# Rotating 96 images by 180 degrees on one core: a group of images is every third image instead of 32 in a row

## The chip, the cores and the metric

The kernel runs on one core of one Trainium2 chip. The metric is the device time of one execution in microseconds. A core has several engines that run side by side; this kernel uses VectorE (DVE in the profile) to copy, SyncE (SP) and ScalarE (ACT) only to issue transfers, and 16 DMA engines that move the bytes between the off-chip memory (HBM, called DRAM in the program) and the on-chip memory (SBUF, 128 partitions).

## The reference

The input is 32 x 3 images of 256 x 256 float32. Each image is turned by 180 degrees, that is, reversed in both of its last dimensions:

```python
batch, c, h, w = 32, 3, 256, 256
return np.rot90(x, k=2, axes=(-2, -1)).astype(np.float32)
```

Seen as a row of 65,536 numbers, an image is simply reversed. 96 images of 256 KB are 25.17 MB, to be read once and written once.

## The kernel before

Each image is cut into 4 quarters of 64 KB (E = 16,384 numbers). A group is 32 images, so it has 128 quarters, one for each SBUF partition. There are three groups, and one buffer for each: A, Bt and Ct (128 x 64 KB each). Partition p holds quarter p modulo 4 of the group's image p // 4.

In the off-chip memory, group 0 is images 0 to 31, group 1 is images 32 to 63, group 2 the rest. The view x4 (lines 37 and 38) joins image and quarter to one dimension of 128 rows, which lie 64 KB apart: a group is one stretch of 8 MB. The view o4 (lines 39 and 40) keeps image and quarter apart, because the store writes the quarters of each image in reversed order (line 59, `::-1`).

The numbers within a quarter are reversed by VectorE in place. `swap` (line 61) exchanges a piece at the left with its mirror piece at the right, in three copies by way of a small buffer T, each reading backwards. A group takes four swaps of 2048 numbers (12 copies of line 52).

The transfers are issued in this order. ScalarE issues the load of the first 512 numbers of each row of A. SyncE issues the load of the rest of A, of Bt, and of Ct, all at the start; line 55 is the call. Then SyncE issues the stores (line 58), each after the copies that it needs: a lead store of the first 128 numbers of each row of A, which can go once the first swap is done; the rest of A; Bt; Ct. VectorE swaps A but for a last piece (1152 numbers), then all of Bt, then A's last piece, then Ct. All DMAs of one issuing engine form one queue, and each of the 16 DMA engines works through its share in order.

Of the kernel before, what the change touches and what calls it, by code (L numbers as in the profile page):

```python
# [2 lines left out]

os.environ.setdefault("NEURON_RT_ULTRASERVER_MODE", "4")

# [4 lines left out]


@with_exitstack
def kernel(
    ctx: ExitStack,
    tc: tile.TileContext,
    x: bass.AP,
    out: bass.AP,
):

    nc = tc.nc
    P = 128

    B, C, H, W = x.shape
    L = H * W
    G = 32
    E = L // 4
    J = E // 8

    x4 = x.rearrange("b c h w -> (b c) (h w)").rearrange(
        "(g n) (s e) -> g (n s) e", n=G, s=4)
    o4 = out.rearrange("b c h w -> (b c) (h w)").rearrange(
        "(g n) (s e) -> g n s e", n=G, s=4)  # L40

    pool = ctx.enter_context(tc.tile_pool(name="slots", bufs=1))
    A = pool.tile([P, E], x.dtype, tag="A")
    Bt = pool.tile([P, E], x.dtype, tag="B")
    Ct = pool.tile([P, E], x.dtype, tag="C")
    T = pool.tile([P, J], x.dtype, tag="T")

    def back(t, lo, hi):
        return t[:, hi - 1:(lo - 1 if lo else None):-1]

    def copy(dst, src):
        tc.keep_in_program_order(nc.vector.tensor_copy(out=dst, in_=src))  # L52

    def load(t, g, lo, hi, queue=nc.sync):
        return queue.dma_start(out=t[:, lo:hi], in_=x4[g][:, lo:hi])  # L55

    def store(t, g, lo, hi):
        return nc.sync.dma_start(
            out=o4[g][:, ::-1, lo:hi], in_=t[:, lo:hi])

    def swap(t, lo, w):
        hi = E - lo - w
        copy(T[:, 0:w], back(t, hi, hi + w))
        copy(t[:, hi:hi + w], back(t, lo, lo + w))
        copy(t[:, lo:lo + w], T[:, 0:w])

    def inside(t):
        for lo in range(0, E // 2, J):
            swap(t, lo, J)

    HEAD = 512
    load(A, 0, 0, HEAD, nc.scalar)
    load(A, 0, HEAD, E)
    load(Bt, 1, 0, E)
    load(Ct, 2, 0, E)
    LAST = 1152
    LEAD = 128
    for lo in range(0, E // 2 - J, J):
        swap(A, lo, J)
    swap(A, E // 2 - J, J - LAST)  # L80
    store(A, 0, 0, LEAD)
    inside(Bt)
    swap(A, E // 2 - LAST, LAST)
    store(A, 0, LEAD, E)
    store(Bt, 1, 0, E)
    inside(Ct)
    store(Ct, 2, 0, E)


# [1 line left out]
_INS = ['x']  # L91
_OUTS = [((32, 3, 256, 256), 'float32')]


# [23 lines left out]
```

## Time and profile before

| what | value |
|---|---|
| median of 3 runs | 121.98 us (121.88 to 122.0) |
| the profiled execution, its time | 122.03 us |
| its span, first to last instruction | 120.2 us |
| VectorE busy | 44.6 us, 37% of the span, 39 copies with 3 waits for loads |
| wait of the first copy of A, of Bt, of Ct for its load | 22.7, 6.1, 1.9 us |
| DMA | 1152 packets, 50.33 MB, 419 GB/s over the span |

The profile's times count from the start of the span. A DMA has an issue, which is the time that an instruction takes on SyncE's or ScalarE's queue, and packets, which are the rows that the DMA engines move afterwards. Here a packet is a row of up to 64 KB. In the slices and windows, a packet counts where it begins, so figures of short stretches scatter around the mean.

### The profile page before, as it was taken

Reading aid. Unit: us, or ns where it says so; the run is one execution under the profiler, and the core shown is the slowest. Engines: PE = TensorE matmul, PEld = TensorE weight load, DVE = VectorE, ACT = ScalarE, POOL = GpSimd, SP = SyncE. Lnnn points to the kernel's source line nnn. Section 1 sums busy time; section 2 is a strip of 40 time slices with the busy share of each in tenths; the row PEclk is TensorE's granted clock in tenths of the full one; section 3 lists DMA queues with packets and bytes.
Section 4 is the critical chain, followed back from the end, with each engine's and each line's share of the span. In section 5 each row is a group of like instructions: output and inputs, shape, how many; then the busy total and the mean of one; then the engine's idle time right before and its main releaser. Section 6 shows DMA issues by size and latency. Waiting matters only on the chain.

```text
span 120.2 us, 98 instructions
## 1 busy us (share of the span) xinstructions
DVE 44.6 (37%) x39; POOL 0.2 (0%) x4
## 2 busy tenths in 40 slices
DVE  0000000499990099999759999400000000000000
POOL 0000000000000000000000000000000000000000
DMA  9888988899889988998889777988898889888980
GB/s 338 349 349 349 698 349 349 360 654 392 349 349 610 436 349 349 589 458 349 349 368 692 346 346 346 692 349 349 349 698 349 349 349 698 349 349 349 676 371 0
DMA packets 1152, 50.33 MB, mean 419 GB/s; under 512 B 128, under 2 KB 256, under 8 KB 384
## 3 DMA queue, kind: packets, MB, share of 16 engines
q1 hardware_dynamic: 1008, 50.07, 96.7%
q10 hardware_dynamic: 144, 0.26, 0.6%
HBM read 25.17 MB, written 25.17 MB: 419 GB/s over the span
## 4 chain that ended last, share of the span: by engine, by line
DMA 34%; DVE 27%; another core or an unknown queue 2%; issue 1%; SPq 0%; DVEq 0%
DMA Bt<-in_x_dram 34%; DVE T L52 9%; DVE Bt L52 8%; DVE Ct L52 8%; DVE A L52 1%; SPq L55 0%; DVEq L52 0%
## 5 line engine op out<-in xcount | busy, mean ns | idle before, releaser
L52 DVE COPY T<-A 128x2048 f32<-128x2048 f32 (+2 forms) x5 | 5.1, 1014 | 22.8 <-DMA A<-in_x_dram 22.7
L52 DVE COPY T<-Bt 128x2048 f32<-128x2048 f32 x4 | 4.9, 1227 | 6.2 <-DMA Bt<-in_x_dram 6.1
L52 DVE COPY T<-Ct 128x2048 f32<-128x2048 f32 x4 | 4.9, 1227 | 2.0 <-DMA Ct<-in_x_dram 1.9
L52 DVE COPY A<-T 128x2048 f32<-128x2048 f32 (+2 forms) x5 | 5.1, 1013 | 0.2
L52 DVE COPY A<-A 128x2048 f32<-128x2048 f32 (+2 forms) x5 | 5.1, 1013 | 0.2
L52 DVE COPY Bt<-T 128x2048 f32<-128x2048 f32 x4 | 4.9, 1227 | 0.1
L52 DVE COPY Ct<-T 128x2048 f32<-128x2048 f32 x4 | 4.9, 1227 | 0.1
L52 DVE COPY Bt<-Bt 128x2048 f32<-128x2048 f32 x4 | 4.9, 1226 | 0.1
L52 DVE COPY Ct<-Ct 128x2048 f32<-128x2048 f32 x4 | 4.9, 1226 | 0.1
L102 POOL MEMSET const-bfloat16-1.0<- 128x1 bf16 x1 | 0.1, 103 | 0.0
L102 POOL MEMSET const-uint8-127<- 128x1 uint8 x1 | 0.1, 103 | 0.0
L102 POOL MEMSET const-float32-1.0<- 128x1 f32 x1 | 0.1, 100 | 0.0
L102 POOL MEMSET const-float32-0.0<- 128x1 f32 x1 | 0.1, 99 | 0.2 <-issue 0.2
## 6 DMA issues: line engine op xcount, KB each, us to landing
out_dram<-A SPq DMA_DIRECT2D x1, 8128.0 KB, 21.2
A<-in_x_dram SPq DMA_DIRECT2D x1, 7936.0 KB, 21.9
A<-in_x_dram ACTq DMA_DIRECT2D x1, 256.0 KB, 22.1
out_dram<-A SPq DMA_DIRECT2D x1, 64.0 KB, 35.2
Bt<-in_x_dram SPq DMA_DIRECT2D x1, 40.8
Ct<-in_x_dram SPq DMA_DIRECT2D x1, 59.8
out_dram<-Bt SPq DMA_DIRECT2D x1, 39.9
out_dram<-Ct SPq DMA_DIRECT2D x1, 42.8
```

The lines of the kernel that those rows point to most:

```text
L52: tc.keep_in_program_order(nc.vector.tensor_copy(out=dst, in_=src))
L102: nc = _bacc.Bacc("TRN2", target_bir_lowering=False, num_devices=1)
```

## The change

A group becomes every third image: group 0 is images 0, 3, 6, and so on, group 1 is 1, 4, 7, group 2 is 2, 5, 8. Both views are changed alike, so what is loaded as one group is stored to its own place again. Consecutive images of a group then lie 768 KB apart instead of 256 KB; the four quarters of an image stay next to each other. Image and quarter can no longer be joined to one dimension of equal steps, so x4 keeps them apart and the load names one dimension more.

```diff
     x4 = x.rearrange("b c h w -> (b c) (h w)").rearrange(
-        "(g n) (s e) -> g (n s) e", n=G, s=4)
+        "(n g) (s e) -> g n s e", n=G, s=4)
     o4 = out.rearrange("b c h w -> (b c) (h w)").rearrange(
-        "(g n) (s e) -> g n s e", n=G, s=4)
+        "(n g) (s e) -> g n s e", n=G, s=4)
...
     def load(t, g, lo, hi, queue=nc.sync):
-        return queue.dma_start(out=t[:, lo:hi], in_=x4[g][:, lo:hi])
+        return queue.dma_start(out=t[:, lo:hi], in_=x4[g][:, :, lo:hi])
```

## The prediction

> **What bounds the kernel now.** I read the busy shares first, then the DMA queues and the windows, then the timeline of the issues, and the chain of waits last. The page (span, busy times, queues):
>
> ```profile
> span 120.2 us, 98 instructions
> DVE 44.6 (37%) x39; POOL 0.2 (0%) x4
> ...
> DMA  9888988899889988998889777988898889888980
> ...
> q1 hardware_dynamic: 1008, 50.07, 96.7%
> q10 hardware_dynamic: 144, 0.26, 0.6%
> HBM read 25.17 MB, written 25.17 MB: 419 GB/s over the span
> ```
>
> VectorE works 37% of the span; the 16 DMA engines carry packets for 96.7 + 0.6 = 97.3% of it. The windows show that their rate has a ceiling and sits on it in both directions (the two late ones hold stores alone):
>
> ```profile
> core 0: us, DVE busy (x) POOL busy (x), PEclk, DMA share, GB/s
> ...
> 63.00:80.00 17.00, 13.26 (x11) 0.00 (x0) 1.00 0.99 428
> 82.00:99.00 17.00, 0.00 (x0) 0.00 (x0) 1.00 1.00 432
> 101.00:118.00 17.00, 0.00 (x0) 0.00 (x0) 1.00 1.00 432
> ```
>
> A packet counts in the slice where it begins, so single windows scatter by a row (16 x 64 KB). The packet records of the trace say it more sharply. The 256 whole 64 KB rows of the loads of Bt and Ct took 2.418 us at the median and 2.419 at the mean; the 256 of the stores of Bt and Ct 2.422 at median and 2.423 at mean, between 2.418 and 2.433. Each engine moves 24 rows in and 24 out: 48 x 2.418 = 116.1 us of 120.2. What is left is the start, a seam between loads and stores, and the end. The timeline (start, duration, engine, instruction):
>
> ```profile
> 0.73 0.38 ACTq L55 DMA_DIRECT2D A<-in_x_dram  x1
> 0.73 0.39 SPq L55 DMA_DIRECT2D A<-in_x_dram  x1
> 1.18 0.43 SPq L55 DMA_DIRECT2D Bt<-in_x_dram  x1
> 1.65 0.43 SPq L55 DMA_DIRECT2D Ct<-in_x_dram  x1
> ...
> 59.62 0.55 SPq L58 DMA_DIRECT2D out_dram<-A  x1
> 60.21 0.59 SPq L58 DMA_DIRECT2D out_dram<-Bt  x1
> 61.50 1.23 DVE L52 COPY T<-Ct 128x2048 f32<-128x2048 f32 x1 [1.92 <-DMA Ct<-in_x_dram]
> ```
>
> The issue of A's load by SyncE runs 0.73 to 1.12; its first packet begins at 1.77, 0.65 later. The store of A is issued at 59.62 to 60.16, and its first packet begins at 60.82, again 0.66 after the issue ended. The last packets of Ct's load end between 60.45 and 61.06, and the 512 B rows of A's lead store (8 per engine, 0.027 each) fill the gap, so the seam costs at most some 0.1 us. The chain of waits, in order of time, has the first issue at its head:
>
> ```profile
> 0.67 0.07 issue
> 0.73 0.39 SPq L55
> 1.12 0.06 issue
> 1.18 40.84 DMA Bt<-in_x_dram
> ```
>
> So a first packet that comes later by d pushes every row, Bt's landing, VectorE's chain to the store of A, and the end by d. The last store is free: it is issued at 76.63, some 22 us before its rows can move.
>
> **The base.** This execution took 122.03 us, 1.78 outside its span of 120.25; the median of the three runs is 121.98. I add to the median; 0.05 is the difference.
>
> **The change part by part.** VectorE's 39 copies, their order, all semaphores, the bytes, and the eight DMAs stay; the built program differs in the four loads and the addresses of the stores.
>
> (a) The form of the loads. The built program has their SBUF side as 128x15872 (128x16384, 128x512) before and as 128x1x15872 and so on after, and their DRAM side as two dimensions before and three after (32 images, 4 quarters, elements). All four stores have that three-dimensional form already, before and after. So the row for a load's issue after the change is a store's: 0.539 and 0.545 us where nothing was issued just ahead, 0.595 right behind another, and 0.632 for the first on SyncE (the lead store at 26.46), against a load's 0.387 for the first and 0.428 and 0.432 behind another. For the first load that is 0.545 - 0.387 = +0.16 at the least and 0.632 - 0.387 = +0.245 at the most. I take +0.24, because this load will be the first instruction of its form on its engine, as the lead store was. The issue is uncovered: nothing moves before it. The issues of Bt and Ct grow by 0.17 each but lie behind A's rows (20 us of queue). ScalarE's HEAD load grows alike; its first 2 KB packet begins at 4.78, after the first 63,488 B packets, though it was issued along with them, so it is hidden; without that cover it would cost the same 0.16 to 0.25 beside SyncE's, not after it.
>
> (b) The start of the stream. The first 16 packets (63,488 B) took 2.897 us on the mean, 2.34 to 3.36, all later ones 2.342: about 0.55 us lost, once. No view says whether that is the memory's first accesses, which the new addresses touch, or the descriptors of the other loads. If the spread rows cure it, -0.55. If it is the issues behind the first that hold it (each 0.17 longer, two of them), +0.34. I take 0, nearest to a load whose packets are of the same size and number.
>
> (c) Steady reading. 2.418 is the floor to the nanosecond; nothing can be gained. A loss has no row of its own; the slowest steady row of a load took 2.442. All 24 rows so: +0.6 us. I take 0.
>
> (d) Steady writing. Rows take 0.004 over the floor: 24 x 0.004 = 0.1 us to gain. Each first 65,024 B packet of A's store took 2.437 on the mean against 2.404 for the rest, so touching new rows costs something; were all store rows at the worst of 2.433: 24 x 0.011 = +0.26. I take 0.
>
> (e) The seam. Bt's landing, the 15 copies behind it and Ct's load keep their distance, so it moves as a block; 0, between -0.1 and +0.1.
>
> Sum: 121.98 + 0.24 = 122.22; I say 122.25, since the open terms lean up (c can only lose).
>
> One rule speaks against the change, and the numbers here do not use it. The Trainium skill, "DMA: Bandwidth & Descriptors", section "Latency and other measured facts", reports copies whose partition rows lie at large power-of-two pitches: at 512 KiB it has 207 GB/s per direction of a full 214, at 2 MiB 164. The trace runs at its ceiling with images 256 KB apart. 768 KB is three times a power of two and keeps only the factor of 256 KB, so I read the rule as no loss; by its 512 KiB row it would be 3.4% of the 116 us of rows, some 4 us, to 126.
>
> **The rivals.** About 0.2% (0.24 us) is what a measurement here can tell from no change.
> - *Issue at its lowest price, all else the same:* +0.16, 122.14, within the bound. For it: the stores at 59.62 and 76.63 pay only 0.54. Against it: neither is a first of its form.
> - *The addresses help (the other side):* the 0.55 of the slow first packets goes. Less 0.24 of issue, plus 0.1 of writing gained: -0.41, 121.57. It decides once the first packets take under 2.42 instead of 2.90 (0.24 regained and 0.24 more). For it: later packets read the same memory in 2.342. Against it: the early packets all end together around 4.8 to 5.3 whatever their start, as if waiting for one event, not for slow memory.
> - *The first data wait for all three issues:* 0.24 + 0.34 = +0.58, 122.56. For it: they end together as just said. Against it: some end their issue long before.
> - *The addresses hurt:* rows of loads at 2.442 and of stores at 2.433 add 0.6 + 0.26: 122.25 + 0.86 = 123.1.
> - *The change does not do what it says:* the trace names no engine and address, so which rows go together is not seen; the issue's price stays, 122.14 to 122.23.
>
> **How the numbers follow.** Forecast with the first load's issue at its upper price: 0.30. Issue at its lower price, or the change without effect on memory: 0.30, which lies within the bound. All three issues: 0.13. Addresses hurt: 0.14. Addresses help: 0.13. The forecast's price is nearly the bound itself; I lay 0.27 of its 0.30 above it and 0.03 within. Slower: 0.27 + 0.13 + 0.14 = 0.54. Same: 0.30 + 0.03 = 0.33. Faster: 0.13. The range leaves out the far half of both address cases: 121.7 to 122.95. The forecast's own range is 122.14 to 122.4.
>
> **What would show it.** In the timeline the first load's issue by SyncE at 0.55 to 0.64 instead of 0.39, the first packet 0.65 after its end, Bt's landing (42.0 now) later by as much as the end. Rows at 2.418 in the loads and about 2.422 in the stores clear the memory; anything above 2.43 convicts it. The first 16 packets at 2.9 keep (b) at nothing. The prediction fails if these rows change, or if the loads' issues stay at 0.39.

## The result and the profile after

The changed kernel takes 122.33 us at the median of ten runs (122.21 to 122.57), against 121.94 for the kernel before in ten runs beside it. The two medians lie 0.39 us apart; the ratio given with the runs is 1.0024, with a 95% interval of 1.0015 to 1.0032, which is 0.18 to 0.39 us: slower by some 0.3 us. A second set of runs, later and beside other kernels, gave 1.0029 (1.0018 to 1.0041). The profiled execution took 122.33 us, 0.30 more than the one of before; its span grew by 0.28, from 120.25 to 120.53.

The page of the changed kernel (span, busy times, queues):

```profile
span 120.5 us, 98 instructions
DVE 44.6 (37%) x39; POOL 0.2 (0%) x4
...
q1 hardware_dynamic: 1008, 50.07, 96.6%
q10 hardware_dynamic: 144, 0.26, 0.6%
HBM read 25.17 MB, written 25.17 MB: 418 GB/s over the span
```

The same work, the same number of packets, the same bytes. In the windows over the later part (length, busy time of VectorE and GpSimd, clock, DMA share, GB/s), DMA share and rate are those of before to the last digit. VectorE has 0.30 us more in the first, because its copies of Ct run later and more of them falls into the window:

```profile
63.00:80.00 17.00, 13.56 (x12) 0.00 (x0) 1.00 0.99 428
82.00:99.00 17.00, 0.00 (x0) 0.00 (x0) 1.00 1.00 432
101.00:118.00 17.00, 0.00 (x0) 0.00 (x0) 1.00 1.00 432
```

In the packet records, the rows of Bt's and Ct's loads took 2.418 us at the median, as before. The rows of their stores took 2.4224 and 2.4240 on the mean, against 2.4220 and 2.4232: 8 rows of each per engine, so 8 x 0.0004 + 8 x 0.0008 = 0.01 us. In the steady rows the new addresses show no cost. The timeline shows what changed (start, duration, engine, instruction):

```profile
0.72 0.64 SPq L55 DMA_DIRECT2D A<-in_x_dram  x1
0.73 0.62 ACTq L55 DMA_DIRECT2D A<-in_x_dram  x1
1.42 0.59 SPq L55 DMA_DIRECT2D Bt<-in_x_dram  x1
2.05 0.60 SPq L55 DMA_DIRECT2D Ct<-in_x_dram  x1
```

All four issues of loads are longer. SyncE's first took 0.643 us instead of 0.387, and the first packet begins at 2.14 instead of 1.77, 0.37 later: 0.256 from the issue, 0.13 because the packet now comes 0.775 after the issue's end instead of 0.648, less 0.01 because this issue began that much earlier. The chain of waits, in order of time, begins with this issue:

```profile
0.66 0.06 issue
0.72 0.64 SPq L55
1.36 0.06 issue
1.42 40.95 DMA Bt<-in_x_dram
```

VectorE's wait for A's load (in total, times, longest) grows from the first line to the second:

```profile
DVE T L52 <- DMA A<-in_x_dram: 22.7, 1, 22.7
DVE T L52 <- DMA A<-in_x_dram: 23.0, 1, 23.0
```

Behind it everything is shifted nearly as a block. By the landing of the last packet (when its completion is signalled), SyncE's load of A comes 0.35 later (22.66 to 23.01), Bt's 0.36, Ct's 0.33, and the last store 0.28 (119.44 to 119.72). The 0.09 us between the first packet and the end stands in a smaller spread of the 16 last rows, which end between 119.21 and 119.37, before between 118.81 and 119.09: on the mean they end 0.38 later, the last of them only 0.28. Why the spread shrank is not known.

### The profile page after: what moved, and what is told of

Same layout as the page of the kernel before. It is cut to its first block, busy times and chain, and to the rows that moved or that the text cites. A ratio compares the mean times of both kernels' runs of the same rounds, so it can differ in the third digit from the quotient of the medians.

```text
span 120.5 us, 98 instructions
## 1 busy us (share of the span) xinstructions
DVE 44.6 (37%) x39; POOL 0.2 (0%) x4
## 4 chain that ended last, share of the span: by engine, by line
DMA 34%; DVE 27%; another core or an unknown queue 1%; issue 1%; SPq 1%; DVEq 0%
DMA Bt<-in_x_dram 34%; DVE T L52 9%; DVE Bt L52 8%; DVE Ct L52 8%; DVE A L52 1%; SPq L55 1%; DVEq L52 0%
```

## The experiments

Two ways in which the change could cost 0.3 us were to be told apart first: the form of the loads (theory 1) and the distance of the images (theory 2). Theory 3 was that the first data wait for all three issues of SyncE. Below, the short form of a DMA has two dimensions on both sides (128 rows, numbers), as the loads before; the long form has three (images, quarters, numbers), as the loads of the changed kernel and all stores.

**Form without distance.**

```diff
-        "(g n) (s e) -> g (n s) e", n=G, s=4)
+        "(g n) (s e) -> g n s e", n=G, s=4)
...
-        return queue.dma_start(out=t[:, lo:hi], in_=x4[g][:, lo:hi])
+        return queue.dma_start(out=t[:, lo:hi], in_=x4[g][:, ::-1, lo:hi])
...
-            out=o4[g][:, ::-1, lo:hi], in_=t[:, lo:hi])
+            out=o4[g][:, :, lo:hi], in_=t[:, lo:hi])
```

> Groups stay 32 images in a row, but the reversal of an image's four quarters moves from the store to the load, so all loads get the three-dimensional form (128x1x15872 and so on) and all stores lose it; same bytes, same rows. Theory 1 (the price is the form of the first load): SyncE's first issue about 0.64 us as in the changed kernel against 0.39, first packet at about 2.1 us against 1.77, time +0.25 to +0.4 us over before. Theory 2 (the price is the distance of the images): no change, within 0.1 us. Theory 3 (all three issues hold the start): as theory 1.

122.35 us, ratio 1.0027 (1.0012 to 1.0042): a loss of the same size, with the images where they were. The wait of VectorE for A in this kernel, in total, times, longest:

```profile
DVE T L52 <- DMA A<-in_x_dram: 23.1, 1, 23.1
```

Before, this wait was 22.7, in the changed kernel 23.0. SyncE's first issue took 0.627 us, the first packet began at 2.13. The stores have the short form here, and their issues shrink from 0.54 to 0.63 us to 0.33 to 0.42 (Bt's and Ct's in the timeline):

```profile
60.42 0.42 SPq L58 DMA_DIRECT2D out_dram<-Bt  x1
77.04 0.33 SPq L58 DMA_DIRECT2D out_dram<-Ct  x1
```

Their rows take 2.419 us on the mean instead of 2.423, some 0.1 us over an engine's 24 rows, so the run's loss may hide that much more.

**Distance without form.**

```diff
     x4 = x.rearrange("b c h w -> (b c) (h w)").rearrange(
-        "(g n) (s e) -> g (n s) e", n=G, s=4)
+        "i (s e) -> (i s) e", s=4).rearrange("(p g) e -> g p e", g=3)
     o4 = out.rearrange("b c h w -> (b c) (h w)").rearrange(
-        "(g n) (s e) -> g n s e", n=G, s=4)
+        "i (s e) -> (i s) e", s=4).rearrange("(n s g) e -> g n s e", n=G, s=4)
```

> Loads in the cheap two-dimensional form, but a group is every third quarter (row pitch 192 KB, so every fourth row, where the 256 KB step was, lies 768 KB on). Stores go to the same rows with the quarter index reversed as before; quarters therefore land in other places than the reference wants, and that part of the computation is changed. Theory 1 (form): first issue 0.39 us, first packet 1.77, time of before within 0.1 us. Theory 2 (distance): +0.25 to +0.4 us, with rows or first packets that take longer than before's 2.418 and 2.90.

122.0 us, ratio 1.0001 (0.9993 to 1.0009): nothing. Its first issues in the timeline are short again:

```profile
0.73 0.37 SPq L55 DMA_DIRECT2D A<-in_x_dram  x1
0.73 0.39 ACTq L55 DMA_DIRECT2D A<-in_x_dram  x1
```

The wait of VectorE for A (in total, times, longest):

```profile
DVE T L52 <- DMA A<-in_x_dram: 22.8, 1, 22.8
```

Whole rows of its loads took 2.418 us at the median and those of its stores 2.422 and 2.425, at a pitch of 192 KB from row to row. Theory 2 is out.

**Which of the issues.** Group A stays in a row; the other two groups take every second image of the remaining 64, so that the images of a group lie 512 KB apart, and their loads have the long form. In the code, xi and oi are views of the images from 32 on:

```diff
+        src = xi[g - 1][:, :, lo:hi] if g else x4[g][:, lo:hi]
+        return queue.dma_start(out=t[:, lo:hi], in_=src)
...
+        dst = oi[g - 1] if g else o4[g]
```

> Group A is images 0 to 31 in a row with the cheap form; Bt and Ct are every second of the other 64 images (512 KB apart) with the three-dimensional form. Theory 1 (first load's form alone): first packet 1.77 us, time of before within 0.1 us, although the issues of Bt and Ct take about 0.59. Theory 2 (distance): two thirds of the loss, +0.2 us or more. Theory 3 (first data wait for all three issues): two issues longer by 0.17, so the first 16 packets end about 0.3 us later and the time is +0.3 us.

121.92 us, ratio 0.9995 (0.9985 to 1.0005). The issues of Bt and Ct took 0.65 us each, and the time is that of before:

```profile
0.72 0.38 SPq L60 DMA_DIRECT2D A<-in_x_dram  x1
0.73 0.39 ACTq L60 DMA_DIRECT2D A<-in_x_dram  x1
1.17 0.65 SPq L60 DMA_DIRECT2D Bt<-in_x_dram  x1
1.87 0.65 SPq L60 DMA_DIRECT2D Ct<-in_x_dram  x1
```

So the loss is with the loads of A; theory 3 is out. Putting off the issues behind A says so from the other side:

```diff
+    nc.gpsimd.memset(Bt[:, 0:4096], 0.0)
     load(Bt, 1, 0, E)
```

> Before with one thing added: GpSimd writes zeros to part of Bt before its load, so the loads of Bt and Ct are issued some microseconds later, when A's rows already move. Theory 3 (the issues behind the first hold up the first packets): the first 16 packets take about 2.35 instead of 2.90 us on the mean and the time falls by up to 0.5 us. Theories 1 and 2 with a start that is slow for the memory's first accesses or for the first load's own descriptors: first 16 packets stay at about 2.9 us, time unchanged within 0.1 us.

122.13 us, ratio 1.0013 (1.0003 to 1.0023): not faster. Bt's issue moved from 1.18 to 4.27. The first 16 packets of SyncE's load did take only 2.47 us on the mean, but in this execution ScalarE's HEAD rows went first, from 1.76, and SyncE's began at 2.05; the shorter packets are no gain. That it was slower than before nobody had expected. GpSimd's writing is not the reason:

```diff
+    nc.gpsimd.memset(T[:, 0:J], 0.0)
+    nc.gpsimd.memset(T[:, 0:J], 0.0)
     load(Bt, 1, 0, E)
```

> Before, with GpSimd writing zeros twice to the small buffer T at the start (about 3.5 us of writing), which no load waits for. The run with late loads of Bt and Ct was 0.13% slower, with its first packet at 2.05 us. If GpSimd's writing beside the first packets was the cause: the same here, first packet at about 2.05 and +0.15 us. If the late issues were the cause: first packet at about 1.75 and the time of before within 0.1 us.

122.04 us, ratio 1.0000 (0.9989 to 1.0010), first packet at 1.74. So the late issues may cost some 0.1 us; the intervals of the two runs overlap. In the profile with the late issues SyncE's load of A lands spread over 0.91 us (22.06 to 22.97), before over 0.46. The cause is left open.

**SyncE's issue or ScalarE's.** A has two loads: HEAD on ScalarE and the rest on SyncE. Each got the long form alone. HEAD alone (x4r keeps image and quarter apart):

```diff
-    load(A, 0, 0, HEAD, nc.scalar)
+    nc.scalar.dma_start(out=A[:, 0:HEAD], in_=x4r[0][:, ::-1, 0:HEAD])
```

> Before, with ScalarE's HEAD load alone in the three-dimensional form (it names the four quarters of each image in reversed order, so the first 512 numbers of A's rows come from the wrong quarter; that part of the computation is changed). Theory 1a (SyncE's first issue alone sets the start): ScalarE's issue 0.62 us, first 63,488 B packet at 1.75 and time of before within 0.1 us. Theory 1b (ScalarE's issue beside it holds the start too): first 16 packets end 0.1 to 0.35 us later than before's mean of 4.99, and the time grows by as much.

121.93 us, ratio 0.9997 (0.9986 to 1.0008): nothing. HEAD's rows began only at 7.05 us here, and VectorE's second copy waited 1.3 us for them; its wait for Bt, 6.1 us before, is shorter by as much:

```profile
DVE T L54 <- DMA Bt<-in_x_dram: 4.9, 1, 4.9
DVE A L54 <- DMA A<-in_x_dram: 1.3, 1, 1.3
```

Then SyncE's alone:

```diff
-    load(A, 0, HEAD, E)
+    nc.sync.dma_start(out=A[:, HEAD:E], in_=x4r[0][:, ::-1, HEAD:E])
```

> Before, with SyncE's first load alone in the three-dimensional form (A from number 512 on, quarters of each image in reversed order; wrong rows there, that part of the computation is changed). HEAD, Bt and Ct keep the cheap form. Theory 1a: SyncE's issue 0.63 us and the whole loss, +0.25 to +0.4 us. Theory 1b: a part of it, +0.1 to +0.2 us, the rest in the run with HEAD's form alone. Theory 3 (later issues matter): less than the whole too, by about 0.3 us.

122.03 us, ratio 1.0005 (0.9994 to 1.0017). Neither form alone costs what both cost together. The transfers of this kernel (KB, us from issue to landing) show what happened:

```profile
A<-in_x_dram SPq DMA_DIRECT2D x1, 7936.0 KB, 21.8
A<-in_x_dram ACTq DMA_DIRECT2D x1, 256.0 KB, 3.0
```

HEAD landed 3.0 us after its issue. Before it took 22.1, because SyncE's rows were there first and HEAD's went between them:

```profile
A<-in_x_dram ACTq DMA_DIRECT2D x1, 256.0 KB, 22.1
```

Here HEAD's rows run from 1.74 on, and SyncE's begin at 2.61. Theory A now says that, of HEAD's and SyncE's, the earlier of the two first issues starts the stream, and that the other has that time as cover; theory B stays with SyncE alone. Since the interval left both open, the run was repeated, beside the changed kernel with HEAD's load in the short (cheap) form, the changed kernel without HEAD, and the changed kernel as it is.

> Before with SyncE's first load alone in the three-dimensional form, once more (numbers of A from 512 on come from the wrong quarter; that part of the computation is changed), because its first interval, 0.9994 to 1.0017, left both open. Theory A: 1.000 to 1.001, HEAD's packets first. Theory B: 1.002 to 1.003.

122.03 us, ratio 1.0008 (0.9999 to 1.0016).

```diff
+    rows = x.rearrange("b c h w -> (b c) (h w)").rearrange(
+        "i (s e) -> (i s) e", s=4).rearrange("(p g) e -> g p e", g=3)
-    load(A, 0, 0, HEAD, nc.scalar)
+    nc.scalar.dma_start(out=A[:, 0:HEAD], in_=rows[0][:, 0:HEAD])
```

> The changed kernel, with ScalarE's HEAD load alone back in the cheap two-dimensional form (it takes the first 512 numbers of every third quarter, so HEAD's numbers come from the wrong rows; that part of the computation is changed). Theory A (the earlier of the two first issues starts the slow beginning, and the other has that time as cover): HEAD's packets from 1.75 us, and a ratio to before of 1.000 to 1.001 instead of the changed kernel's 1.0024. Theory B (SyncE's first issue alone): 1.002 to 1.003.

121.89 us, ratio 1.0000 (0.9991 to 1.0009). All of the loss is gone, though SyncE's first issue is as long as in the changed kernel (timeline):

```profile
0.72 0.64 SPq L55 DMA_DIRECT2D A<-in_x_dram  x1
0.72 0.36 ACTq L74 DMA_DIRECT2D A<-in_x_dram  x1
1.42 0.59 SPq L55 DMA_DIRECT2D Bt<-in_x_dram  x1
2.05 0.60 SPq L55 DMA_DIRECT2D Ct<-in_x_dram  x1
```

VectorE's wait for A is half a microsecond shorter than the changed kernel's 23.0:

```profile
DVE T L52 <- DMA A<-in_x_dram: 22.5, 1, 22.5
```

And HEAD lands 2.6 us after its issue (KB, us to landing; the changed kernel's line stands below it):

```profile
A<-in_x_dram ACTq DMA_DIRECT2D x1, 256.0 KB, 2.6
A<-in_x_dram ACTq DMA_DIRECT2D x1, 256.0 KB, 22.5
```

HEAD's packets begin at 1.72, SyncE's at 2.58. The HEAD rows are 8 per engine at 0.084 us, so 0.67 us of work that has to be done at some time. Done here, it fills the time in which SyncE's issue is late.

> The changed kernel once more, beside the others: ratio to before 1.002 to 1.0035 under every theory; first packet at about 2.14 us.

122.28 us, ratio 1.0029 (1.0018 to 1.0041), apart from the interval of the cheap HEAD beside it. In this execution too HEAD's packets came first, but from 2.15: with both issues long, the first packet was as late whichever queue went first.

> The changed kernel without HEAD: SyncE loads all of A in one DMA, in the three-dimensional form. Theory A and theory B alike: first packet at 2.0 to 2.15 us, ratio 1.002 to 1.0035. If the 0.13 us that the first packet came later than the longer issue alone explains is due to two such issues at once: first packet at 2.02 (issue end + 0.65) instead of 2.14.

122.46 us, ratio 1.0047 (1.0034 to 1.0060), first packet at 2.17, 0.77 after the issue's end. So the extra 0.13 us does not come from two long issues at once. Leaving out HEAD (`load(A, 0, 0, E)` in place of both loads) costs more than expected here; its interval overlaps that of the run with HEAD, so how much is open. The same edit in the kernel before:

> Before without ScalarE's load: SyncE loads all of A in one DMA. If two issues at once are what makes the first 16 packets take 2.90 instead of 2.34 us: they take about 2.5 and the time falls by 0.2 to 0.5 us. If they take as long as before (about 2.9 to 3.0 for 65,536 B), the start has another cause and the time is that of before within 0.15 us.

122.08 us, ratio 1.0007 (0.9995 to 1.0020). The first 16 packets took 3.16 us on the mean (65,536 B; later ones 2.42), so the slow start is there with one issue too.

| kernel | SyncE's, ScalarE's first issue, us | first packet, us | ratio to before |
|---|---|---|---|
| before | 0.387, 0.383 | 1.77 | 1 |
| changed, two sets of runs | 0.643, 0.624 (0.657, 0.612) | 2.14 (2.15) | 1.0024, 1.0029 |
| form without distance | 0.627, 0.622 | 2.13 | 1.0027 |
| distance without form | 0.372, 0.386 | 1.73 | 1.0001 |
| A in a row, Bt and Ct in the long form | 0.382, 0.392 | 1.74 | 0.9995 |
| before, loads of Bt and Ct late | 0.398, 0.387 | 1.76 | 1.0013 |
| before, GpSimd writes T | 0.379, 0.397 | 1.74 | 1.0000 |
| before without HEAD | 0.387, none | 1.74 | 1.0007 |
| changed without HEAD | 0.667, none | 2.17 | 1.0047 |
| form in HEAD alone | 0.379, 0.581 | 1.74 | 0.9997 |
| form in SyncE's load of A alone | 0.653, 0.373 | 1.74 | 1.0005, 1.0008 |
| changed, HEAD cheap | 0.643, 0.363 | 1.72 | 1.0000 |

The loss goes with the first packet of either queue: where it came at 2.13 us or later, the kernel is 0.24 to 0.47% slower; where it came by 1.77, only the run with late loads has an interval wholly above 1 (1.0003 to 1.0023). The size is not explained in full: without HEAD the loss is larger at nearly the same first packet. No version was shown to beat the kernel before.

## Why the prediction was right, and where it was not

The direction, the range and the cause held: 122.25 was forecast, 122.33 measured. That the loss exceeds the 0.2% which the prediction took for its bound is not shown: both intervals begin below it. How near the number came is partly luck, as the first two points show.

- *Step (a), the form.* The mechanism was right; the run with the form alone and the run with the distance alone show it. The size was short. The lead store's 0.632 was the right row for the issue (0.643 measured, +0.256 against +0.245), but the reason given for it, the first instruction of its form on its engine, is not borne out: in the changed kernel the lead store follows three loads of that form on SyncE and still took 0.616, and with A in a row Ct's load, the second of its form among the loads, took 0.649. The step also took the first packet to come 0.65 after the issue's end, as behind the store of A; it came 0.775 after, a term of 0.13 that was missing. In the profile +0.37 at the first packet became +0.28 at the end, so most of the missing term did not reach the end; the ratio of the first set makes 0.0024 x 121.94 = 0.29.
- *"The issue is uncovered: nothing moves before it."* This is the step that failed. It counted SyncE's issue as the price and ScalarE's as hidden. Yet with HEAD's issue short, HEAD's packets do move before SyncE's, from 1.72 to 1.75 us, and cover it: the time is lost only where neither queue has a short first issue. HEAD's long issue alone costs nothing, SyncE's alone 0.05 to 0.08% (both intervals hold no change), and with HEAD cheap the changed kernel shows no loss (1.0000, 0.9991 to 1.0009). The sum came out near because the change lengthens both.
- *Step (b), the start.* 0 was right. The first 16 packets took 3.07 instead of 2.90 us, but on the mean they end 0.38 later (5.37 for 4.99), as much as the first packet is late. Their duration is no sign of a loss: it was 3.11 us with the distance alone and 3.14 with GpSimd writing, both at the time of before, and 2.94 with the form alone, at the full loss. The rival in which the first data wait for all three issues falls with the run that has A's loads alone in the cheap form: longer issues of Bt and Ct, no loss. Without HEAD and with GpSimd busy the first packets stayed slow (3.16 and 3.14); in the profiles in which HEAD's went ahead, SyncE's first 16 took 2.47 to 2.64. What makes them slow was not found.
- *Steps (c) and (d), the memory.* 0 was right: loads at 2.418, stores 0.01 us longer in sum. The Trainium skill's rule on row pitches at large powers of two ("DMA: Bandwidth & Descriptors", section "Latency and other measured facts") lists pitches from 512 KiB on. The 126 us that the prediction worked out by its 512 KiB row did not come. Here images 256 KB and 768 KB apart and quarters 192 KB apart all ran at the same row time, and so did the images 512 KB apart in the run with A in a row (2.418 for loads). Rows at the pitches of its table were not tried, for an image's quarters lay 64 KB apart there. The sign "anything above 2.43" was too sharp: single rows of loads, the last ahead of the seam, took up to 2.547 before and 2.444 after. And the reading in (d) that touching new rows costs something does not hold: with the form moved to the loads, A's store writes to the same places in the short form and in forward order, and its first packets took 2.400 on the mean instead of 2.437.
- *Step (e), the seam.* 0 was right: the first packet of A's store moved by 0.39 us (60.82 to 61.21), as the first packet of all did by 0.37.
- *The rivals in which the addresses help or hurt* both fall with the distance alone: 1.0001.

What makes an issue long is not settled by these runs. The DMAs that were cheap (the short loads, and the stores of the run with the form alone) have two dimensions on both sides, and in the built program they alone carry a mark for a prepared form; no run here separates the mark from the dimensions.

## What to carry to other kernels

When a kernel's transfers run at their ceiling from the first packet to the last, look for time to win or lose ahead of the first packet and behind the last; here a shift of the first packet was nearly the whole effect. Rewriting an index changes more than addresses: look at the shape of each DMA in the built program, because a view that no longer joins to one row dimension can lengthen the issue, here from 0.39 to 0.64 us. Here it mattered only at the head of the stream (longer issues of Bt and Ct cost nothing, shorter issues of the stores won nothing that was seen), and there a small load in the short form on another queue covered it.

## What was not expected of the hardware

- The first packet of a load in the long form came 0.77 to 0.80 us after the end of its issue, in the short form 0.62 to 0.65 (in the profiles where its queue went first), while the first packet of A's store, in the long form too, came 0.66 after its issue. The cause is open.
- With both first issues nearly equally long, which queue's packets go first differed between executions: in the changed kernel SyncE's rows went first in one profile, and HEAD's in the other (there HEAD's begin at 2.15 and SyncE's at 3.00). The two profiled executions took 122.33 and 122.16 us.
- Putting off the loads behind the first by 3.1 us, though they had 20 us to spare, seems to have made the kernel slower by 0.13% (0.03 to 0.23%), though the interval overlaps that of the run in which GpSimd only writes. The landings of A's load spread twice as wide, 0.91 against 0.46 us, but a spread of 0.68 went with no loss in the run with the distance alone. The cause is open.
